# A token copy scaled by routing weights: four output pools become one output tile used in regions

## The chip, the cores and the metric

The kernel runs on one core of a Trainium2 chip. The metric is device time in microseconds (us) of one execution, as the median of several runs. One more execution of each kernel was recorded by the hardware profiler; all profile lines here come from such executions, and times in them are counted from the start of the span.

Three engines matter. VectorE (DVE) and ScalarE (ACT) compute. SyncE (SP) computes nothing here; it issues transfers. Transfers run on 16 DMA engines, fed by two queues in this kernel: ScalarE's queue (q10 in the profile) loads x, SyncE's queue (q1) loads the weights and stores the results.

## The reference

```python
def reference(x, expert_indices, expert_weights):
    batch, seq, hidden = x.shape              # 16, 1024, 512, float32
    k = expert_indices.shape[-1]              # 2
    x_expanded = x[:, :, np.newaxis, :].repeat(k, axis=2)
    weights = expert_weights[..., np.newaxis]
    return (x_expanded * weights).astype(np.float32)
```

Every token has a row of 512 numbers and two weights, and the result holds the row twice, once times each weight. The expert indices are used for their shape only. 33.6 MB of x and 0.1 MB of weights go in, and 67.1 MB come out.

## The kernel before

There are 16,384 tokens, which is 128 rows of tokens for each of the 128 partitions. The kernel works on five tiles of 25 token rows (`groups`) and a remainder of 3 (`LAST`). In a tile each partition holds 25 consecutive tokens, so a partition's part of a transfer is one contiguous run in memory: 2 KB per row of input and 4 KB per row of output.

*Loads.* `load` brings a tile of x into one of two buffers (`x_pool`). Tile 0 comes in five loads of 4, 4, 5, 8 and 4 rows; the others come in one load of 25 rows. The three loads of weights are issued on SyncE's queue beside the first three loads of x; the last three rows of x (`z_tile`) are loaded behind tile 0. Tiles 0 and 1 are loaded at the start, and tile i+2 after the products of tile i have been written into the program. As these loads stand on ScalarE's queue, they are issued in order with ScalarE's products, and they wait until both engines have read the old tile in that buffer.

*Products.* `product` has two forms. On VectorE one TENSOR_TENSOR instruction makes up to four rows (`CH`), with x and the weights both broadcast. On ScalarE one ACTIVATE makes half an output row: 512 numbers times one weight. For the first two pieces of tile 0 a third form splits single half-rows between ScalarE and VectorE (`nc.any`), two of three to VectorE as TENSOR_SCALAR.

*Stores.* Each tile is made in four pieces of 7, 6, 6 and 6 rows (`PIECES`). Piece h is written to a tile of its own pool, `o_pools[h]`, each with one buffer; VectorE makes the first four rows, ScalarE the others, and SyncE then stores the piece. So piece h of the next tile can be filled only when the store of piece h of this tile has landed. The remainder uses the buffer of piece 0 and is stored last, in a transfer of 3 rows. In all there are 21 stores, 10 loads of x and 3 of weights.

The framework places the waits: an instruction waits for the semaphores of what last wrote or read its bytes. Each engine runs its own instructions in program order.

Of the kernel before, what the change touches and what calls it, by code (L numbers as in the profile page):

```python
# [1 line left out]

# [4 lines left out]


@with_exitstack
def kernel(  # L10
    ctx: ExitStack,
    tc: tile.TileContext,
    x: bass.AP,
    expert_indices: bass.AP,
    expert_weights: bass.AP,
    out: bass.AP,
):
    nc = tc.nc

    batch, seq, hidden = x.shape  # L20
    k = expert_weights.shape[-1]
    P = nc.NUM_PARTITIONS
    ntok = batch * seq
    assert ntok % P == 0
    A_TOTAL = ntok // P

    f32 = mybir.dt.float32
    row = k * hidden
    CH = 4


    groups = [25, 25, 25, 25, 25]
    TX = max(groups)
    LAST = 3
    assert sum(groups) + LAST == A_TOTAL

    xf = x.rearrange("b s h -> (b s) h")
    of = out.rearrange("b s k h -> (b s) (k h)")
    wf = expert_weights.rearrange("b s k -> (b s) k")

    w_pool = ctx.enter_context(tc.tile_pool(name="w_pool", bufs=1))
    x_pool = ctx.enter_context(tc.tile_pool(name="x_pool", bufs=2))
    o_pools = [
        ctx.enter_context(tc.tile_pool(name=f"o_pool{h}", bufs=1)) for h in range(4)
    ]

    w_tile = w_pool.tile([P, A_TOTAL * k], f32)

    def rows(of_all, done, T):
        return of_all[done * P : (done + T) * P, :].rearrange(  # L50
            "(p a) n -> p (a n)", a=T
        )


    if LAST:
        z_pool = ctx.enter_context(tc.tile_pool(name="z_pool", bufs=1))
        z_tile = z_pool.tile([P, LAST * hidden], f32)

    tiles = []
    done = 0  # L60
    for n in groups:
        tiles.append((done, n))
        done += n

    loaded = []

    def load(i):
        if i >= len(tiles):
            return
        done, n = tiles[i]  # L70
        x_tile = x_pool.tile([P, TX * hidden], f32)
        src = rows(xf, done, n)
        steps = [4, 4, 5, 8, 4] if i == 0 else [n]
        for e, step in enumerate(steps):
            at = sum(steps[:e])
            nc.scalar.dma_start(
                out=x_tile[:, at * hidden : (at + step) * hidden],
                in_=src[:, at * hidden : (at + step) * hidden],
            )
            if i == 0 and e < 3:  # L80
                weights(e)
        if i == 0 and LAST:
            nc.scalar.dma_start(out=z_tile, in_=rows(xf, A_TOTAL - LAST, LAST))  # L83
        loaded.append(x_tile)


    T0 = groups[0]
    G = len([n for n in groups[1:] if n == T0])
    head = (1 + G) * T0

    def weights(e):
        if e == 0:
            nc.sync.dma_start(out=w_tile[:, : T0 * k], in_=rows(wf, 0, T0))
        elif e == 1:
            nc.sync.dma_start(
                out=w_tile[:, T0 * k : head * k].rearrange("p (g n) -> p g n", g=G),
                in_=wf[T0 * P : head * P, :].rearrange(
                    "(g p a) n -> p g (a n)", g=G, p=P
                ),
            )  # L100
        else:
            nc.sync.dma_start(
                out=w_tile[:, head * k :], in_=rows(wf, head, A_TOTAL - head)
            )

    def product(engine, o_tile, t, x_in, c, m):

        o = t * row
        if engine is not None:
            for e in range(m * k):  # L110
                out_e = o_tile[:, o + e * hidden : o + (e + 1) * hidden]
                in_e = x_in[:, e // k * hidden : (e // k + 1) * hidden]
                w_e = w_tile[:, c + e : c + e + 1]
                if engine is nc.scalar or engine is nc.any and (c + e) % 3 == 2:
                    nc.scalar.mul(out=out_e, in_=in_e, mul=w_e)  # L115
                else:
                    nc.vector.tensor_scalar(  # L117
                        out=out_e,
                        in0=in_e,
                        scalar1=w_e,  # L120
                        scalar2=None,
                        op0=mybir.AluOpType.mult,
                    )
            return
        nc.vector.tensor_tensor(  # L125
            out=o_tile[:, o : o + m * row].rearrange(
                "p (t k h) -> p t k h", t=m, k=k
            ),
            in0=x_in[:, : m * hidden]
            .rearrange("p (t h) -> p t h", t=m)  # L130
            .unsqueeze(2)
            .to_broadcast([P, m, k, hidden]),
            in1=w_tile[:, c : c + m * k]
            .rearrange("p (t k) -> p t k", t=m)
            .unsqueeze(3)
            .to_broadcast([P, m, k, hidden]),
            op=mybir.AluOpType.mult,
        )

    def make(i, e, o_tile, x_in, c, m):  # L140
        if i == 0 and e < 2:
            product(nc.any, o_tile, 0, x_in, c, m)
            return
        v = min(m, CH)
        product(None, o_tile, 0, x_in, c, v)
        if m > v:
            product(nc.scalar, o_tile, v, x_in[:, v * hidden :], c + v * k, m - v)

    PIECES = [7, 6, 6, 6]
    for i in range(2):  # L150
        load(i)
    for i, (done, n) in enumerate(tiles):
        x_tile = loaded[i]
        outr = rows(of, done, n)
        at = 0
        for h, m in enumerate(PIECES):
            o_tile = o_pools[h].tile([P, m * row], f32)
            make(
                i,
                h,  # L160
                o_tile,
                x_tile[:, at * hidden : (at + m) * hidden],
                (done + at) * k,
                m,
            )
            nc.sync.dma_start(out=outr[:, at * row : (at + m) * row], in_=o_tile)  # L166
            at += m
        load(i + 2)
    if LAST:
        o_tile = o_pools[0].tile([P, PIECES[0] * row], f32)  # L170
        product(None, o_tile, 0, z_tile, (A_TOTAL - LAST) * k, LAST)
        nc.sync.dma_start(
            out=rows(of, A_TOTAL - LAST, LAST), in_=o_tile[:, : LAST * row]
        )

# [1 line left out]
_INS = ['x', 'expert_indices', 'expert_weights']  # L177
_OUTS = [((16, 1024, 2, 512), 'float32')]


# [23 lines left out]
```

## Time and profile before

| what | us |
|---|---|
| median of 3 runs | 240.68 |
| the 3 runs | 240.57, 240.68, 242.03 |
| the profiled execution | 240.69 |
| its span in the profile | 238.9 |
| VectorE busy | 90.3 |
| ScalarE busy | 57.3 |

The span goes from the first to the last instruction that the profiler recorded; the 1.8 us between it and the execution's time lie outside. The page counts as busy only instructions that compute. The DMA rows give the mean share of the 16 DMA engines that had a packet under way, and the bytes moved. A packet is counted in the stretch in which it is seen, so a short stretch can show a share above 1.00 and a rate that jumps; long stretches are to be read.

The store queue of this kernel issues its first store at 16.28 us and the last one, of 3 rows, at 215.68 us.

### The profile page before, as it was taken

The numbers are of one execution on the slowest core, as the hardware profiler recorded it, in microseconds if no ns is written. First come the engines' busy times: TensorE is split into PE (matmuls) and PEld (weight loads), VectorE is DVE, ScalarE is ACT, GpSimd is POOL, SyncE is SP. The second block draws the span as 40 slices with busy tenths as digits, with TensorE's granted clock in tenths as the row PEclk, the third lists the DMA queues.
The fourth block names the chain that finished last, engine by engine and source line by source line (L and its number), as shares of the span: only waits on it lengthen the run. The fifth ranks groups of instructions, "written<-read, shape, count | busy, mean of one in ns | idle before, by whom it ended". The sixth has DMA issues, their size and how long they took to land.

```text
span 238.9 us, 260 instructions
## 1 busy us (share of the span) xinstructions
DVE 90.3 (38%) x37; ACT 57.3 (24%) x89; POOL 0.2 (0%) x4
## 2 busy tenths in 40 slices
DVE  0769300060074557000775260035575556741000
ACT  0747000060034226000444150042245423400000
POOL 0000000000000000000000000000000000000000
DMA  6999999899899999999999999999999999999995
GB/s 242 428 409 413 445 441 460 383 457 483 378 438 399 460 418 447 424 440 430 411 444 447 494 406 406 414 429 436 433 437 428 432 440 429 446 418 428 432 426 245
DMA packets 5281, 100.80 MB, mean 422 GB/s; under 512 B 1312, under 2 KB 1312, under 8 KB 1440
## 3 DMA queue, kind: packets, MB, share of 16 engines
q1 hardware_dynamic: 3840, 67.24, 65.5%
q10 hardware_dynamic: 1440, 33.56, 33.0%
q14 instruction: 1, 0.01, 0.0%
HBM read 33.69 MB, written 67.11 MB: 422 GB/s over the span
## 4 chain that ended last, share of the span: by engine, by line
DMA 81%; DVE 9%; issue 0%; ACTq 0%; DVEq 0%; SPq 0%
DMA out_dram<-o_tile 60%; DMA x_tile<-in_x_dram 20%; DVE o_tile L125 9%; ACTq L83 0%; DVEq L125 0%; SPq L166 0%
## 5 line engine op out<-in xcount | busy, mean ns | idle before, releaser
L125 DVE TENSOR_TENSOR o_tile<-x_tile,w_tile 128x4096 f32<-128x4096 f32 x18 | 79.6, 4425 | 113.6 <-DMA out_dram<-o_tile 87.7
L115 ACT ACTIVATE o_tile<-x_tile,w_tile 128x512 f32<-128x512 f32 x88 | 56.0, 709 | 142.2 <-DMA out_dram<-o_tile 110.9
L117 DVE TENSOR_SCALAR o_tile<-x_tile,w_tile 128x512 f32<-128x512 f32 x18 | 7.4, 481 | 7.7 <-DMA x_tile<-in_x_dram 7.7
L125 DVE TENSOR_TENSOR o_tile<-z_tile,w_tile 128x3072 f32<-128x3072 f32 x1 | 3.4, 3358 | 4.1 <-DMA out_dram<-o_tile 4.1
L115 ACT ACT_TABLE_LOAD x1 | 1.3, 1283 | 6.9 <-DMA x_tile<-in_x_dram 6.9
L188 POOL MEMSET const-bfloat16-1.0<- 128x1 bf16 x1 | 0.1, 102 | 0.0
L188 POOL MEMSET const-uint8-127<- 128x1 uint8 x1 | 0.1, 102 | 0.0
L188 POOL MEMSET const-float32-1.0<- 128x1 f32 x1 | 0.1, 99 | 0.0
L188 POOL MEMSET const-float32-0.0<- 128x1 f32 x1 | 0.1, 98 | 0.2 <-issue 0.2
## 6 DMA issues: line engine op xcount, KB each, us to landing
out_dram<-o_tile SPq DMA_DIRECT2D x15, 3072.0 KB, 40.8
x_tile<-in_x_dram ACTq DMA_DIRECT2D x4, 6400.0 KB, 35.2
out_dram<-o_tile SPq DMA_DIRECT2D x5, 3584.0 KB, 36.9
x_tile<-in_x_dram ACTq DMA_DIRECT2D x3, 1024.0 KB, 7.6
x_tile<-in_x_dram ACTq DMA_DIRECT2D x1, 2048.0 KB, 15.0
out_dram<-o_tile SPq DMA_DIRECT2D x1, 1536.0 KB, 21.9
x_tile<-in_x_dram ACTq DMA_DIRECT2D x1, 1280.0 KB, 10.5
z_tile<-in_x_dram ACTq DMA_DIRECT2D x1, 768.0 KB, 20.6
```

The lines of the kernel that those rows point to most:

```text
L115: nc.scalar.mul(out=out_e, in_=in_e, mul=w_e)
L117: nc.vector.tensor_scalar(out=out_e, in0=in_e, scalar1=w_e, scalar2=None, op0=mybir.AluOpType.mult,)
L125: nc.vector.tensor_tensor(out=o_tile[:, o : o + m * row].rearrange("p (t k h) -> p t k h", t=m, k=k), in0=x_in[:, : m * hidden] .rearrange ...
L188: nc = _bacc.Bacc("TRN2", target_bir_lowering=False, num_devices=1)
```

## The change

One tile `o_ring` of 25 output rows takes the place of the four pools, with the same bytes in all. Each tile of x writes its results at the same row numbers of `o_ring`, cut into pieces (`cuts`): rows 0 to 12 and 13 to 24 for the first two tiles, rows 0 to 8, 9 to 16 and 17 to 24 for the three others. The remainder is written to rows 0 to 2. That makes 14 stores in place of 21.

In each piece VectorE now makes about two thirds of the rows, in steps of up to four, and ScalarE the last third: 9 + 4 rows and 8 + 4 rows in the first two tiles; 6 + 3, 6 + 2 and 6 + 2 in the others; 2 + 1 in the remainder. The split by half-rows in tile 0 is gone.

Tile 0 is loaded in two transfers of 9 and 16 rows in place of five; the three loads of weights keep their order on SyncE's queue. There are 7 loads of x in place of 10, and 24 transfers in all in place of 34.

```diff
+    FIRST = [9, 16]
...
-    o_pools = [
-        ctx.enter_context(tc.tile_pool(name=f"o_pool{h}", bufs=1)) for h in range(4)
-    ]
+    o_pool = ctx.enter_context(tc.tile_pool(name="o_pool", bufs=1))
...
+    o_ring = o_pool.tile([P, TX * row], f32)
...
-        steps = [4, 4, 5, 8, 4] if i == 0 else [n]
+        steps = FIRST if i == 0 else [n]
...
-            if i == 0 and e < 3:
-                weights(e)
+            if i == 0 and e == 0:
+                for g in range(3):
+                    weights(g)
...
-    def make(i, e, o_tile, x_in, c, m):
-        if i == 0 and e < 2:
-            product(nc.any, o_tile, 0, x_in, c, m)
-            return
-        v = min(m, CH)
-        product(None, o_tile, 0, x_in, c, v)
-        if m > v:
-            product(nc.scalar, o_tile, v, x_in[:, v * hidden :], c + v * k, m - v)
+    def fill(o_tile, x_in, c, m):
+        v = m - m // 3
+        for t in range(0, v, CH):
+            u = min(t + CH, v)
+            product(None, o_tile, t, x_in[:, t * hidden : u * hidden], c + t * k, u - t)
+        product(nc.scalar, o_tile, v, x_in[:, v * hidden :], c + v * k, m - v)

-    PIECES = [7, 6, 6, 6]
+    def emit(src, dst, c, cuts):
+        for at, to in zip(cuts, cuts[1:]):
+            o_tile = o_ring[:, at * row : to * row]
+            fill(o_tile, src[:, at * hidden : to * hidden], c + at * k, to - at)
+            nc.sync.dma_start(out=dst[:, at * row : to * row], in_=o_tile)
+
     for i in range(2):
         load(i)
     for i, (done, n) in enumerate(tiles):
...
-        for h, m in enumerate(PIECES):
-            o_tile = o_pools[h].tile([P, m * row], f32)
-            make(
...
-            )
-            nc.sync.dma_start(out=outr[:, at * row : (at + m) * row], in_=o_tile)
-            at += m
+        cuts = [0, 13, n] if i < 2 else [0, 9, 17, n]
+        emit(loaded[i], rows(of, done, n), done * k, cuts)
         load(i + 2)
-    if LAST:
-        o_tile = o_pools[0].tile([P, PIECES[0] * row], f32)
-        product(None, o_tile, 0, z_tile, (A_TOTAL - LAST) * k, LAST)
-        nc.sync.dma_start(
-            out=rows(of, A_TOTAL - LAST, LAST), in_=o_tile[:, : LAST * row]
-        )
+    emit(
+        z_tile,
+        rows(of, A_TOTAL - LAST, LAST),
+        (A_TOTAL - LAST) * k,
+        [0, LAST],
+    )
```

More of the change, by code (lines that the diff above doesn't have):

```diff
@@ L152 @@
     for i, (done, n) in enumerate(tiles):
-        x_tile = loaded[i]
-        outr = rows(of, done, n)
-        at = 0
-        for h, m in enumerate(PIECES):
-            o_tile = o_pools[h].tile([P, m * row], f32)
-            make(
[L159 to L164, printed above, removed]
-            )
-            nc.sync.dma_start(out=outr[:, at * row : (at + m) * row], in_=o_tile)
-            at += m
-        load(i + 2)
-    if LAST:
-        o_tile = o_pools[0].tile([P, PIECES[0] * row], f32)
-        product(None, o_tile, 0, z_tile, (A_TOTAL - LAST) * k, LAST)
-        nc.sync.dma_start(
-            out=rows(of, A_TOTAL - LAST, LAST), in_=o_tile[:, : LAST * row]
-        )
+        cuts = [0, 13, n] if i < 2 else [0, 9, 17, n]
+        emit(loaded[i], rows(of, done, n), done * k, cuts)
+        load(i + 2)
+    emit(
[4 more added lines that the diff above has]
+    )
 _INS = ['x', 'expert_indices', 'expert_weights']
```

## The prediction

> **What bounds the kernel now.** I read the first page from the top: busy shares, the slices, the bytes, the chain of waits.
>
> ```profile
> span 238.9 us, 260 instructions
> DVE 90.3 (38%) x37; ACT 57.3 (24%) x89; POOL 0.2 (0%) x4
> DMA  6999999899899999999999999999999999999995
> ...
> q1 hardware_dynamic: 3840, 67.24, 65.5%
> q10 hardware_dynamic: 1440, 33.56, 33.0%
> ...
> HBM read 33.69 MB, written 67.11 MB: 422 GB/s over the span
> ...
> DMA 81%; DVE 9%; issue 0%; ACTq 0%; DVEq 0%; SPq 0%
> ```
>
> No compute engine is busy half the time. The DMA row holds nines and eights but for the two edges, and the queues' packets fill 65.5 + 33.0 = 98.5% of 16 engines' span. The waits say the same from the other side: VectorE and ScalarE wait for stores to leave, and the store queue waits for VectorE.
>
> ```profile
> ACT o_tile L115 <- DMA out_dram<-o_tile: 110.9, 15, 18.4
> DVE o_tile L125 <- DMA out_dram<-o_tile: 91.7, 16, 17.9
> ...
> SPq L166 <- DVE o_tile L125: 184.6, 18, 27.8
> ```
>
> That last row looks like compute holding stores back. It is not: while SP waits, earlier stores are still in flight. Windows decide it (columns: stretch, length, busy time of three engines, PE clock, DMA share, GB/s).
>
> ```profile
> 0.00:2.00 2.00, 0.00 (x0) 0.00 (x0) 0.20 (x4) 1.00 0.20 25
> 2.00:3.00 1.00, 0.00 (x0) 0.00 (x0) 0.00 (x0) 1.00 0.60 181
> 4.00:16.00 12.00, 7.39 (x18) 6.40 (x9) 0.00 (x0) 1.00 1.02 420
> 20.00:60.00 40.00, 10.37 (x3) 5.98 (x10) 0.00 (x0) 1.00 1.02 442
> 20.00:235.00 215.00, 80.11 (x19) 48.05 (x76) 0.00 (x0) 1.00 1.00 433
> 234.00:236.00 2.00, 0.00 (x0) 0.00 (x0) 0.00 (x0) 1.00 1.01 430
> 236.00:237.00 1.00, 0.00 (x0) 0.00 (x0) 0.00 (x0) 1.00 0.44 184
> ```
>
> From 20 to 235 us the share is 1.00 at 433 GB/s. So the span is the bytes at 433 GB/s (100.80 MB: 232.8 us) plus some 6.1 us of edges and of a slower start. The bytes are the same after the change. The time can move only if the DMA runs dry somewhere, if its rate changes, or if the edges do.
>
> **The change, part by part.** Units first: one token row of output for all partitions is 524,288 bytes, 1.21 us at 433 GB/s; one of input is half, 0.605 us.
>
> *Compute.* The rows that price it:
>
> ```profile
> L125 DVE TENSOR_TENSOR o_tile<-x_tile,w_tile 128x4096 f32<-128x4096 f32 x18 | 79.6, 4425 | 113.6 <-DMA out_dram<-o_tile 87.7 <-DMA x_tile<-in_x_dram 25.9
> ...
> L117 DVE TENSOR_SCALAR o_tile<-x_tile,w_tile 128x512 f32<-128x512 f32 x18 | 7.4, 481 | 7.7 <-DMA x_tile<-in_x_dram 7.7
> ...
> L115 ACT ACT_TABLE_LOAD x1 | 1.3, 1283 | 6.9 <-DMA x_tile<-in_x_dram 6.9
> ```
>
> ```profile
> 0.73 2.85 ACTq L76 DMA_DIRECT2D x_tile<-in_x_dram  x5
> 6.02 2.46 DVE L117 TENSOR_SCALAR o_tile<-x_tile,w_tile 128x512 f32<-128x512 f32 x6 [6.02 <-DMA x_tile<-in_x_dram]
> 16.28 192.34 SPq L166 DMA_DIRECT2D out_dram<-o_tile  x20
> 49.58 3.78 ACT L115 ACTIVATE o_tile<-x_tile,w_tile 128x512 f32<-128x512 f32 x6 [27.38 <-DMA x_tile<-in_x_dram]
> ```
>
> VectorE makes four rows in 4.43 us, 1.11 a row; ScalarE makes six half-rows in 3.78 us, 0.63 each, 1.26 a row. After the change VectorE makes 17 rows of each of the first two tiles, 18 of each later one and 2 of the last three: 90 rows, 100 us. ScalarE makes 38 rows, 48 us. Both stay far under the span, so only the places count where a store waits for them.
>
> *The start.* The first load grows from 4 rows to 9. Four rows landed at 6.02, so nine land at 6.0 + 5 x 0.605 = 9.1, and the other sixteen at 18.8. VectorE's nine rows run from 9.1 to 19.0. ScalarE's first rows need the second load: 18.8 + 1.28 (table) + 8 x 0.63 gives 25.1. So the first store leaves at about 25.2 where it left at 16.28: 9 us later. What hides this is the load queue: x tile 0, the last three rows and x tile 1 are 53 input rows, 32.1 us, issued on ScalarE's queue ahead of its products. From 2.6 us on they last until about 34.7, so there are 9.5 us to spare; with that cover gone, each us of a later store would cost one.
>
> *The start's rate.* 4 to 16 us ran at 420 rather than 433 GB/s, a loss of 12 x 13/433 = 0.36 us. The row allows two readings. If the small first loads cause it, two loads in place of five give up to 0.36 us back. If reading without stores causes it, reading alone lasts 9 us longer and costs 9 x 13/433 = 0.27 us. I take zero, between them. The Trainium skill ("DMA: Bandwidth & Descriptors", in its section on the iDMA fabric) measured a load stream alone at 408.7 GB/s; by that figure the longer reading would cost an estimated 0.5 us. The trace's 420 lies above it and decides.
>
> *Packets.* Loads are 10 transfers and q10 holds 10 x (128 + 16) = 1440 packets: one for each partition's whole run, and one per engine at the end. Ten transfers fewer are 1440 packets fewer, 90 on each engine.
>
> ```profile
> q1 hardware_dynamic: 787, 0.13, 4.4%
> ...
> q10 hardware_dynamic: 150, 6.81, 65.7%
> q1 hardware_dynamic: 148, 3.49, 33.7%
> ```
>
> The first row is from 0 to 17 us, where q1 carries the tiny weight packets: 0.044 x 17 x 16 / 787 = 15 ns each. So at most 90 x 15 ns = 1.35 us go. The other two rows, from 26 to 50 us, say that it is less: loads (51 KB a packet) make 6.81 MB in 0.657 of 24 us, 432 GB/s, stores (24 to 28 KB) 3.49 MB in 0.337, also 432. A price of 15 ns on each would part these rates by 0.7%. I take 0.2 us off, nearer to that row, and keep 0 and 1.35 for the range.
>
> *Shares and loads.* In that window 150 load packets alternate with 148 store packets, so each queue's share goes by packet size. Store packets grow to 53 and 49 KB beside loads of 51 KB: loads fall from two thirds of the rate to half. Working forward row by row at 433 GB/s, x tiles 1 to 4 land near 44, 74, 121 and 161 us. The regions that they fill come free at about 57, 101, 138 and 183, so every load stays at least 13 us early.
>
> *The regions.* Three in place of four (two at first) mean fewer stores queued while the next is made. A region's fill starts when the store that held it has landed, and must end before what is still queued runs out. From a load's issue to its landing goes 5.3 us (0.73 to 6.02), of which 4 rows' data take 2.4; so a hand-over costs 2.9 us at most beside the fill. The two tightest places are those without a load in flight:
> - Tile 1's second piece, about 81 us: one store of 13 rows is queued, 15.7 us, and the fill of 8 rows takes 8.9. That leaves 6.9, and after the 2.9, 4.0 us.
> - Tile 2's second piece, about 127 us. Its last rows overlap the old 12-row region, so they wait for that store. Nine rows are queued, 10.9 us; two rows on either engine take 2.6. That leaves 8.3, and 5.4.
>
> Elsewhere two stores or a load stand behind. So SP's longer waits at each store cost nothing, and nothing else is queued behind them on SP. ScalarE's queue also carries the x loads, each behind the products of the tile before: issued about 3 us later than now (near 90 and 136 us in place of 86.96 and 132.63), which the 13 us cover.
>
> ```profile
> 86.96 0.36 ACTq L76 DMA_DIRECT2D x_tile<-in_x_dram  x1
> ...
> 132.63 0.35 ACTq L76 DMA_DIRECT2D x_tile<-in_x_dram  x1
> ```
>
> *The end.* The last three rows wait for the first region of tile 4; then 16 rows, 19.4 us, are still queued, and two rows on VectorE take 2.2. The last store is of the same size, so the tail (data until 236.5, the end at 238.9) stays.
>
> *Sum.* The profiled execution took 240.69, 1.8 above its span and equal to the median of 240.68. 240.69 + 0 - 0.2 = 240.5.
>
> **The rivals.**
> 1. *The queue runs dry at the two tight hand-overs (slower).* It decides when a landing and re-issue take over 6.9 us in place of 2.9, which engines out of step would do, since a store lands with its slowest engine. At 10 us the places lose 3.1 + 1.7: 245.3. For it: only one store is in flight there. Against it: at the end all engines stop between 236 and 237 us, so they keep within 1 us.
> 2. *Long store packets move more slowly (slower).* No store above 28 KB a packet is in the trace. At 420 GB/s, the lowest rate above, 67.11 MB take 4.8 us longer: 245.3. Against it: loads of 51 KB run at the stores' rate.
> 3. *A gap at each transfer goes (faster).* The rate of 442 from 20 to 60 us, held for all 215, would save 4.4 us: 236.3. The Trainium skill ("DMA: Bandwidth & Descriptors", on the anatomy of one DMA) gives about 2.0 us fixed for a transfer on the GpSimd path; ten in series would be 20 us, 220.7. That sum the trace refutes here, because transfers overlap. In the last stage the fills, each begun by a landing, follow at 7.28 and 7.26 us, and 6 rows in 7.26 us are 433 GB/s with no room for a gap:
>
> ```profile
> 189.25 2.56 ACT L115 ACTIVATE o_tile<-x_tile,w_tile 128x512 f32<-128x512 f32 x4 [3.44 <-DMA out_dram<-o_tile]
> ...
> 196.53 2.56 ACT L115 ACTIVATE o_tile<-x_tile,w_tile 128x512 f32<-128x512 f32 x4 [4.72 <-DMA out_dram<-o_tile]
> ...
> 203.79 2.56 ACT L115 ACTIVATE o_tile<-x_tile,w_tile 128x512 f32<-128x512 f32 x4 [4.69 <-DMA out_dram<-o_tile]
> ```
>
> 4. *The tile is not tracked by regions.* Then each fill would wait for all stores, and the DMA would idle for it: nine pieces of tiles 2 to 4 at 6.6 us of fill and 2.9 us each are 86 us, of which two loads of 15.1 us cover 30: 296. The built program's waits speak against it: each fill waits for the store that held its own rows.
>
> **How the numbers follow.** Within 1% (238.3 to 243.1, about what a measurement of this kernel can tell from no change) is the forecast, 0.80. Rival 1 has 0.08, rival 2 0.05, rival 3 0.06, rival 4 0.01. So faster 0.06, same 0.80, slower 0.14. The forecast alone reaches from 240.7 - 1.35 - 0.36 = 239.0 to 240.7 + 0.27 = 241.0; the runs of before reached 242.0, so I end at 242.2. Outside lie the rivals, 0.20 at most.
>
> **What would show it.** The DMA row should stay at nines, with 1.00 of DMA share from 20 to 235 us; VectorE near 100 us busy, ScalarE near 48; the first store at 25 us; 3841 packets; x loads issued near 30, 90 and 136 us. A slice of 7 or less near 96 or 137 us would be rival 1. A rate other than 433 GB/s at a share of 1.00 would be rival 2 or 3.

## The result, and the profile after

The changed kernel takes 239.86 us (median of 13 runs, 239.59 to 240.33) where the kernel before takes 241.42 (13 runs, 240.41 to 242.53). The ratio is 0.9938, with a 95% interval of 0.9919 to 0.9956. Run again beside the experiments it took 239.89 against 240.73: 0.9959, interval 0.9940 to 0.9978. It is faster by about half a per cent, which the many runs tell from zero though it is under the 1% of the forecast. The fastest executions of the two differ by 0.82 us (240.41 and 239.59); the medians differ by 1.56, because the kernel before varies more, up to 242.53. What its longer executions lose is not shown: the one that was profiled took 240.69. Where a kernel below had executions more than 1.5% above its fastest, they are counted in its median but left out of its ratio.

The page of the changed kernel, with the rows that answer to those shown of before:

```profile
span 237.8 us, 214 instructions
DVE 99.1 (42%) x29; ACT 49.1 (21%) x77; POOL 0.2 (0%) x4
DMA  7999999999999999999999999999999999999996
...
q1 hardware_dynamic: 2832, 67.24, 65.7%
q10 hardware_dynamic: 1008, 33.55, 33.2%
...
DMA 68%; DVE 20%; issue 2%; ACT 1%; DVEq 0%; SPq 0%
```

Nines from edge to edge, 98.9% of the span in packets, VectorE at 99 and ScalarE at 49 us: the kernel is bound as before. The chain's share of VectorE rose from 9% to 20%, and yet the DMA share stays at 1.00: a chain through an engine is no loss while other transfers are queued. The windows (stretch, length, three engines' busy time, PE clock, DMA share, GB/s):

```profile
4.00:16.00 12.00, 7.11 (x2) 0.00 (x0) 0.00 (x0) 1.00 1.05 447
20.00:60.00 40.00, 7.50 (x2) 9.98 (x17) 0.00 (x0) 1.00 1.01 428
20.00:235.00 215.00, 88.00 (x26) 47.94 (x77) 0.00 (x0) 1.00 1.00 431
26.00:50.00 24.00, 1.50 (x1) 3.99 (x7) 0.00 (x0) 1.00 0.98 413
```

These rates need care. The view counts a packet whole where it is seen, and here the engines run in step: one load packet more or less on each of the 16 is 0.82 MB, or 34 GB/s over 24 us. With each packet shared out over its recorded time, 4 to 16 us have 430 GB/s (418 before) and 26 to 50 us 426 (433 before), so both differences are smaller than the rows make them. The stretch from 26 to 50 us shows something else that was not expected. First the queues from 26 to 50 us (packets, MB, share), then the weights' loads (KB, us from issue to landing):

```profile
q10 hardware_dynamic: 209, 9.88, 97.6%
q1 hardware_dynamic: 209, 0.02, 0.7%
```

```profile
w_tile<-in_expert_weights_dram SPq DMA_DIRECT2D x1, 100.0 KB, 36.8
w_tile<-in_expert_weights_dram SPq DMA_DIRECT2D x1, 25.0 KB, 5.3
w_tile<-in_expert_weights_dram SPq DMA_DIRECT2D x1, 3.0 KB, 50.4
```

The stores' queue moved 0.02 MB in 24 us, though its first store had been issued at 25.12. Equal packet counts say why: an engine takes one packet from each queue in turn. The records show it directly: every 1.90 us each engine starts one load packet and one tiny packet. (The Trainium skill, "DMA: Bandwidth & Descriptors", section on queues, rings and completion order, has engines go round their queues in this way, switching only after a whole packet; by that rule, the 209 beside 209 agrees.) The weights are 768 packets of 24 and 200 bytes, 48 on each engine, and stand ahead of the stores. Each waits for a load packet of up to 51 KB. Before, tile 0 came in many short packets, and the same three loads landed 3.9, 15.0 and 17.4 us after their issue. Now 3 KB take 50.4 us, and no store moves until then. The engines do not run dry meanwhile, because the load queue stays full that long: tile 2 of x was issued at 30 us.

Where the 1.1 us between the two profiled spans (of executions of 240.69 and 239.60) went follows from the records of single packets. The median durations are:

```
bytes in a packet    12288   24576   28672   32768   49152   51200   53248
ns                     460     912    1062    1213    1815    1891    1966
9 ns + bytes at 27.22 GB/s
                       460     912    1062    1213    1815    1890    1965
```

So each packet costs 9 ns beside its bytes, and without that the 16 engines would move 436 GB/s. (The Trainium skill gives 435 GB/s as the ceiling, in the specifications of "DMA: Bandwidth & Descriptors"; the records agree.) Summed over the 16 engines and divided by 16, in us:

```
                                            before   after
first packet starts                           1.74    1.72
packets' time, mean of the engines          235.50  235.09
gaps between packets                          0.05   -0.14
last packet ends                            237.29  236.67
last landing                                237.62  237.01
from it to the end of the span                1.29    0.81
```

(A gap below zero means that packets overlap a little.) The packets' time fell by 0.4: 80 data packets and 10 completions fewer at 9 ns are -0.8. The rest is packets that took longer than the rule. The load of the last three rows gives -0.4: before, its packets took 286 ns in the mean for 235 by the rule, mostly between 18 and 20 us, where the stores start. Load packets of 51 KB give +0.7: from 20 to 48 us, without stores, they took 1,899 ns for 1,890, which is 0.1 in all, but the last one on each engine, just ahead of the first store, took 2,420 ns (0.5 us), and some from 96 to 108 us the rest. Tiny packets give +0.1, tile 0's loads nothing. The gaps give another -0.2 and the end of the program -0.5. These parts are read from two executions; no run below takes out one alone and shows it in the time.

### The profile page after: what moved, and what is told of

The parts are those of the page before. It is cut to its first block, busy times and chain, and to the rows that moved or that the text cites. A ratio compares the mean times of both kernels' runs of the same rounds, so it can differ in the third digit from the quotient of the medians.

```text
span 237.8 us, 214 instructions
## 1 busy us (share of the span) xinstructions
DVE 99.1 (42%) x29; ACT 49.1 (21%) x77; POOL 0.2 (0%) x4
## 4 chain that ended last, share of the span: by engine, by line
DMA 68%; DVE 20%; issue 2%; ACT 1%; DVEq 0%; SPq 0%
DMA out_dram<-o_ring 65%; DVE o_ring L126 20%; DMA x_tile<-in_x_dram 3%; ACT o_ring L116 1%; DVEq L126 0%; SPq L152 0%
## 5 line engine op out<-in xcount | busy, mean ns | idle before, releaser
L126 DVE TENSOR_TENSOR o_ring<-x_tile,w_tile 128x4096 f32<-128x4096 f32 (+2 forms) x28 | 96.8, 3507 | 113.0 <-DMA out_dram<-o_ring 99.9
L116 ACT ACTIVATE o_ring<-x_tile,w_tile 128x512 f32<-128x512 f32 x74 | 46.5, 708 | 139.2 <-DMA out_dram<-o_ring 130.8
L116 ACT ACT_TABLE_LOAD x1 | 1.3, 1283 | 18.8 <-DMA x_tile<-in_x_dram 18.8
L126 DVE TENSOR_TENSOR o_ring<-z_tile,w_tile 128x2048 f32<-128x2048 f32 x1 | 2.3, 2292 | 4.3 <-DMA out_dram<-o_ring 4.3
L116 ACT ACTIVATE o_ring<-z_tile,w_tile 128x512 f32<-128x512 f32 x2 | 1.3, 713 | 8.3 <-DMA out_dram<-o_ring 8.3
```

Of the source, the lines that this page charges most:

```text
L126: nc.vector.tensor_tensor(out=o_tile[:, o : o + m * row].rearrange("p (t k h) -> p t k h", t=m, k=k), in0=x_in[:, : m * hidden] .rearrange ...
```

## The experiments

Times in this section are medians; each ratio is against executions of the kernel before that were taken beside it, so ratios are to be compared rather than times of different groups of runs.

**Tile 0 in two loads, alone** (in the kernel before)

```diff
-        steps = [4, 4, 5, 8, 4] if i == 0 else [n]
+        steps = [9, 16] if i == 0 else [n]
...
-            if i == 0 and e < 3:
-                weights(e)
+            if i == 0 and e == 0:
+                for g in range(3):
+                    weights(g)
```

> The kernel before with tile 0 in two loads (9 and 16 rows) and the weights' loads issued behind the first of them; pools, pieces and the 21 stores stay. The start (larger first packets): the 4 to 16 us stretch rises from 420 to about 447 GB/s and nearly the whole gain appears, about 0.9 to 1.5 us less than before. The number of stores: at most 0.3 us of gain. The order of reading and writing (in the changed kernel the weights' tiny packets alternate with large load packets, so stores begin only at 50 us and reads and writes hardly overlap until then): the same gain as by the start, since stores are held back here too; the inline run parts the two.

Measured: 240.75 us against 240.70, ratio 0.9988 (0.9968 to 1.0007). No gain that can be told. Yet the row from 4 to 16 us did rise to 446 GB/s (430 shared out, as in the changed kernel), and the stores were held back too (the first landed at 60.36 us):

```profile
4.00:16.00 12.00, 4.84 (x12) 5.07 (x7) 0.00 (x0) 1.00 1.04 446
...
26.00:50.00 24.00, 4.05 (x1) 0.00 (x0) 0.00 (x0) 1.00 0.98 413
```

The 413 is 426 when shared out, again as in the changed kernel. By the records the load of the last three rows is 0.4 us shorter here than in the kernel before, and the last load packet of each engine ahead of the first store takes 2,391 ns, which costs 0.5. So the start and the order of reading and writing, taken together, are not the gain; the run does not part them. The engines stay in step: the first store's landings are 0.84 us apart, the last one's 0.64.

**Five loads in the changed kernel**

```diff
-    FIRST = [9, 16]
+    FIRST = [4, 4, 5, 8, 4]
...
-            if i == 0 and e == 0:
-                for g in range(3):
-                    weights(g)
+            if i == 0 and e < 3:
+                weights(e)
```

> The changed kernel with tile 0 in the five loads of before (4, 4, 5, 8, 4 rows, weights beside the first three). The start: the gain is lost, about 1 us slower than the changed kernel (some 240.9 to 241.4), first stretch back at 420 GB/s. The number of stores: gain kept, about 239.9. The order of reading and writing: lost too, as stores begin near 25 us.

Measured: 252.35 us, ratio 1.0463 (1.0416 to 1.0511). No theory had foreseen a loss of 12 us. Its page and windows:

```profile
span 249.7 us, 216 instructions
```

```profile
26.00:50.00 24.00, 0.00 (x0) 0.00 (x0) 0.00 (x0) 1.00 0.99 383
96.00:102.00 6.00, 5.37 (x2) 1.54 (x3) 0.00 (x0) 1.00 0.80 346
20.00:235.00 215.00, 86.17 (x26) 42.39 (x68) 0.00 (x0) 1.00 0.99 415
```

Two things are to be seen. From 26 us on the share is full and the rate is 383 (384 shared out): packets take longer. Near 100 us the share itself falls to 0.80: some engines have nothing to do. Two rows from 40 to 50 us show the first: 36 load packets in 0.478 of 16 x 10 us are 2.12 us each, where 1.89 is the rule.

```profile
q10 hardware_dynamic: 36, 1.84, 47.8%
q1 hardware_dynamic: 34, 1.81, 45.1%
```

The completion records show the second. Each transfer completes once per engine; this is when the first and the last of the 16 engines completed it, in us:

```
                     first store     second store    third store     last store
changed kernel       66.79 - 67.60   81.28 - 82.11   98.97 -101.58  236.31 -237.01
five loads           50.68 - 57.62   80.82 - 92.51   98.41 -113.39  243.65 -248.73
kernel before        35.57 - 43.13   57.92 - 65.45   74.41 - 75.08  236.70 -237.62
```

With five loads the engines are 7 to 15 us out of step on these stores, and 5 us at the end. A store lands with its slowest engine, so the next fill starts late, and the engines that are ahead run dry. In the sums, packets take 241.8 us of each engine (8.0 above the rule, 1.5 in the changed kernel) and 4.9 us are gaps. Of these some 3.0 lie at the end, where engines are done before the slowest (0.3 in the changed kernel). The kernel before is out of step by 7.5 us at first, is back within 0.7 us at its third store, and shows no such loss.

**Four pieces in the changed kernel**

```diff
-        cuts = [0, 13, n] if i < 2 else [0, 9, 17, n]
+        cuts = [0, 7, 13, 19, n]
```

> The changed kernel with the four pieces of before (7, 6, 6, 6 rows) for every tile: 21 stores in place of 14. The start and the order: gain kept, within 0.2 us of the changed kernel, about 239.9. The number of stores: seven more, each 0.1 to 0.2 us, so about 1 us slower, near 240.9.

Measured: 243.09 us, ratio 1.0076 (1.0048 to 1.0104). The number of stores explains at most 0.6 us of the 3.2 above the changed kernel (56 packets and 7 completions at 9 ns). The rest again is out of step: the weights' last 3 KB landed at 36.27 us on the first engine and at 52.57 on the last, and the last store's landings are 3.8 us apart. At the end the engines are done 2.9 us before the slowest in the mean, for 0.3 in the changed kernel, which is most of the loss. But the sizes alone do not do it: the run with two loads alone has the same loads, 21 stores of the same sizes and the same weights ahead of them. There the weights' last 3 KB landed at 51.23 us on the first engine and at 51.97 on the last, and the time was 240.75. Its four pools, its split of the work and the first store's issue (13.19 us there, 14.53 here) differ; which of them decides was not tested.

**Weights off the stores' queue, in the changed kernel** (`queue` is the engine that `weights` now issues from)

```diff
-            if i == 0 and e == 0:
-                for g in range(3):
-                    weights(g)
+            if i == 0 and e == 0:
+                weights(0, nc.sync)
+            if i == 0 and e == 1:
+                weights(1, nc.scalar)
+                weights(2, nc.scalar)
```

> The changed kernel with the second and third loads of weights issued on ScalarE's queue behind tile 0's second load, so that no tiny packets stand ahead of the stores. The first store then moves data from about 25 us on, not from 50, and lands near 57 in place of 67.6. The start: time unchanged, about 239.9. The order of reading and writing: the gain shrinks, about 0.5 to 1.5 us slower than the changed kernel.

Measured: 240.49 us, ratio 0.9980 (0.9959 to 1.0001). The first store landed at 60.14, so it did move early. Whether the time rose against the changed kernel is not clear: this interval lies just above the first one of the changed kernel (0.9919 to 0.9956) and overlaps the second (0.9940 to 0.9978). Long loads and long stores alternate here from 25 us on, with all engines within 0.9 us until 82 us, and the rate is 423 GB/s from 26 to 50 us, shared out. So early long stores alone are not what cost 12 us.

**The changed kernel again**

> The changed kernel itself, as the mark for the others of this call: about 0.8 to 1.5 us under the kernel before.

Measured: 239.89 us, ratio 0.9959 (0.9940 to 0.9978), as expected.

**Without the third form of products** (in the kernel before)

```diff
-        if i == 0 and e < 2:
-            product(nc.any, o_tile, 0, x_in, c, m)
-            return
```

> The kernel before without the third form of products: all pieces of tile 0 are made as in the other tiles, so VectorE has 21 instructions of products in place of 37; all transfers stay. In the traces so far the time from the last landing to the span's end is 1.28 and 1.23 us where the third form is used and 0.77 to 0.98 us where it is not; VectorE's last instruction comes late. The end of the program: about 0.4 us less than before, near 240.3, with that stretch at 0.8 us. If it is the number of transfers or the ring that shortens the end, the time stays at 240.7 and the stretch at 1.25 us.

Measured: 240.46 us, ratio 0.9990 (0.9966 to 1.0013), and 0.9 us from the last landing to the end. This fits the theory, but a later run (each store in two) breaks it: that kernel keeps the third form and also ends 0.9 us after its last landing. In the kernel before and in the run with two loads alone, VectorE's very last instruction is late by some 0.35 us; why only there stays open.

**Five loads, weights off the stores' queue** (the five loads of above, and the second and third loads of weights on ScalarE's queue behind the third of them)

```diff
-    FIRST = [9, 16]
+    FIRST = [4, 4, 5, 8, 4]
...
+            if i == 0 and e == 2:
+                weights(1, nc.scalar)
+                weights(2, nc.scalar)
```

> The changed kernel with tile 0 in five loads (252.35 us so far), and with the second and third loads of weights on ScalarE's queue behind tile 0's third load, so that no tiny packets stand on the stores' queue. Engines out of step (the tiny packets leave the 16 engines at different places when the first store comes, and long load and store packets then hold each other up): the loss of 12 us goes, time 239.9 to 240.8, and all engines land a transfer within about 1 us. Early long stores beside loads, whatever the engines' order: still about 250 us.

Measured: 241.56 us, ratio 1.0020 (0.9997 to 1.0042), with ten executions from 240.27 to 242.36 and two at 252.99 and 253.83. Most of the loss went, so the tiny packets are a part of its cause, but not the whole: the engines still get out of step as soon as the first store comes (its landings are 5.3 us apart in an execution of 241.03), and two executions of twelve lost as much as before. The profiled one ran at 431 GB/s from 26 to 50 us, shared out, so long packets out of step are not slow as such. Why two executions lost is not shown, since neither was profiled.

**Each store of the kernel before in two**

```diff
-            nc.sync.dma_start(out=outr[:, at * row : (at + m) * row], in_=o_tile)
+            half = (m + 1) // 2
+            nc.sync.dma_start(
+                out=outr[:, at * row : (at + half) * row], in_=o_tile[:, : half * row]
+            )
+            nc.sync.dma_start(
+                out=outr[:, (at + half) * row : (at + m) * row],
+                in_=o_tile[:, half * row :],
+            )
```

> The kernel before with each of the 20 stores of pieces issued as two transfers: 41 stores in place of 21, so 160 more packets on each engine. Packet records of the traces fit 9 ns plus bytes at 27.2 GB/s for each packet. The price of a packet: 160 x 9 ns = 1.4 us slower than before, near 242.1. No price (packets overlap): no change, 240.7. A price for each transfer of 0.1 us or more: 2 us slower or more.

Measured: 243.12 us, ratio 1.0084 (1.0056 to 1.0112), so 2.0 us by the ratio. The packets' time rose from 235.5 to 238.8: 160 packets and 20 completions at 9 ns are 1.6, and load packets above the rule 1.55 more; smaller gaps and a shorter end gave 1.1 back. The price is there, and each packet's duration is the rule's; the sum of 1.4 was too small, since it left out the load packets, which took longer here. Why they did was not tested.

**Five loads, first store late**

```diff
-    FIRST = [9, 16]
+    FIRST = [4, 4, 5, 8, 4]
...
-    def emit(src, dst, c, cuts):
-        for at, to in zip(cuts, cuts[1:]):
-            o_tile = o_ring[:, at * row : to * row]
+    def emit(src, dst, c, cuts, up=0):
+        for at, to in reversed(list(zip(cuts, cuts[1:]))):
+            o_tile = o_ring[:, (at + up) * row : (to + up) * row]
...
+        up=TX - LAST,
```

> The changed kernel with tile 0 in the five loads of before, and with the pieces of every tile stored in reversed order (rows 13 to 24 first, and the last three rows made in ring rows 22 to 24). So the loads are those of the run at 252.35 us, but the first store waits for the last of them and starts near 26 us, when the queue of loads moves the long packets of tile 1. The first store meeting short load packets is the cause: 239.8 to 240.8 us, engines land the first stores within 1 us of each other. The five loads as such are the cause: near 252, or some executions there.

Measured: 240.69 us, ratio 0.9974 (0.9950 to 0.9998). Ten executions lie between 239.79 and 241.57, two at 244.39 and 244.81; none is near 252. One of the two was profiled, and even there the first store, issued at 25.89, landed on all engines within 0.33 us and the second within 0.47. Its loss came after 90 us. So the five loads as such do not make the loss; it takes an early first store as well. What this store meets is not parted here: at 25.89 us the short load packets are past, and so are the tiny packets, whose last landed at 18.45. The run with five loads and the weights off the stores' queue gives the tiny packets the larger part. An early store beside short loads may add that a small difference between engines is one packet or two, and so a whole store of 53 KB more or less; that was argued, not measured.

**Four pieces, weights off the stores' queue**

```diff
-        cuts = [0, 13, n] if i < 2 else [0, 9, 17, n]
+        cuts = [0, 7, 13, 19, n]
...
+            if i == 0 and e == 1:
+                weights(1, nc.scalar)
+                weights(2, nc.scalar)
```

> The changed kernel with the four pieces of before (243.09 us so far), and with the second and third loads of weights on ScalarE's queue, so that the first store, made at about 15 us, is not held back behind tiny packets. Tiny packets holding stores back at different lengths on different engines cost the 3 us: near 240.6, which is the changed kernel plus 56 packets of 9 ns and 7 completions. Smaller stores with two loads cost them in another way: it stays near 243.

Measured: 241.10 us, ratio 1.0006 (0.9987 to 1.0025): 2.0 us less than with the weights on the stores' queue (1.7 by the ratios), 0.5 above the expectation. Holding stores back behind tiny packets, unequally on different engines, was most of those 3 us. Here two of the early stores land 10.3 us apart, and that costs little, since the engines come back: from 81 us on no transfer's landings are more than 3.5 us apart, and the last store's are 1.6.

**Two pieces for all tiles**

```diff
-        cuts = [0, 13, n] if i < 2 else [0, 9, 17, n]
+        cuts = [0, 13, n]
```

> The changed kernel with two pieces (13 and 12 rows) for all five tiles: 11 stores in place of 14. The price of a packet: 24 data packets and 3 completions fewer on each engine, 0.25 us less, about 239.6. A hand-over that runs dry: the reserve by the prediction's rows is 14.5 us queued less 10.0 us of fill less 2.9 us, 1.6 us, at each of six hand-overs of tiles 2 to 4; if it is overrun the time rises by the overrun at each, 1 us or more in all.

Measured: 240.13 us, ratio 0.9961 (0.9940 to 0.9982), the same as the changed kernel. The packets' time is 234.80, 0.2 to 0.3 less, as expected, but gaps (0.3 us in place of about none) and a longer end of the program (1.0 us in place of 0.8) take it back. No hand-over ran dry:

```profile
20.00:235.00 215.00, 84.34 (x23) 51.30 (x82) 0.00 (x0) 1.00 1.00 430
```

**The regions alone** (five loads and four pieces in the changed kernel)

```diff
-    FIRST = [9, 16]
+    FIRST = [4, 4, 5, 8, 4]
...
-        cuts = [0, 13, n] if i < 2 else [0, 9, 17, n]
+        cuts = [0, 7, 13, 19, n]
```

> The changed kernel with tile 0 in five loads and with the four pieces of before, so that of the change only the one tile used in regions and the split of a piece between the engines are left. It completes a square: two loads with large pieces 239.9, two loads with four pieces 243.1, five loads with large pieces 252.4. The size of the stores makes the run at 252 (load packets of 51 KB alternating with store packets of 49 and 53 KB, out of step): here, with store packets of 24 and 28 KB, 240.3 to 241.0, as before. The regions or the split make it: 245 or more.

Measured: 240.73 us, ratio 0.9987 (0.9959 to 1.0015). With five loads and four pieces, regions and split cost nothing. The square, in us:

```
                  4 pieces (24 and 28 KB)   2 and 3 pieces (32 to 53 KB)
five loads               240.73                     252.35
two loads                243.09                 239.86, 239.89
```

In the kernel with regions neither half of the change gains by itself: against the upper left one loses 2.4 and the other 11.6 (2.1 and 11.5 by the ratios). Together they gain. The square does not hold for the four pools, where two loads with four pieces took 240.75: the sizes alone do not decide whether the engines get out of step.

## Why the prediction was right

It said 240.5, 239.0 to 242.2, and no change beyond 1%; it was 239.86, a change of 0.6% by the ratio. The mechanism was right: the same bytes through DMA engines that stay full. Of what it left out, 0.6 us are in its term for packets and 0.5 at the end of the program. Step by step:

- *The bound.* Right. The share is 1.00 from 20 to 235 us before and after, so compute, waits and the number of regions do not show in the time.
- *Compute and the start.* Right to 0.3 us: the first nine rows landed at 8.89 (9.1), the other sixteen at 18.7 (18.8), the first store left at 25.12 (25.2), and the loads of tiles 2 to 4 at 30.02, 91.04 and 136.53 (30, 90, 136).

```profile
8.89 18.61 DVE L126 TENSOR_TENSOR o_ring<-x_tile,w_tile 128x4096 f32<-128x4096 f32 x5 [8.89 <-DMA x_tile<-in_x_dram]
...
25.12 191.68 SPq L152 DMA_DIRECT2D out_dram<-o_ring  x14
30.02 0.37 ACTq L76 DMA_DIRECT2D x_tile<-in_x_dram  x1
...
91.04 0.36 ACTq L76 DMA_DIRECT2D x_tile<-in_x_dram  x1
...
136.53 0.35 ACTq L76 DMA_DIRECT2D x_tile<-in_x_dram  x1
```

- *The cover of the late store.* The conclusion held, its working did not. It counted 9.5 us to spare between the first store at 25.2 and the end of the loads at 34.7. In fact stores moved nothing before 50 us, and what covered them was tile 2's load, issued at 30.02, before tile 1's landed at 36.05. The step had priced the weights' loads by their own time and not by their place ahead of the stores. The cover had to last 25 us longer than worked out, and that it did was luck.
- *The start's rate.* Zero was close, but neither reading of the 420 GB/s holds. The loads of tile 0 took 0.49 us more than the packet rule before and 0.46 after. Loads of 51 KB without stores beside them took 1,899 ns for 1,890, 0.1 us in all. The 420 is mostly the price of packets: by the rule, packets of 8 to 16 KB run at 423 to 429 GB/s, and 665 packets under 512 bytes took 0.6 us of each engine in that stretch. What moved was at the point where the stores start: 0.4 us gone in the load of the last three rows, 0.5 us new in the last load packet ahead of the first store.
- *Packets.* Mis-sized. It took 0.2 us off; 80 data packets and 10 completions at 9 ns are 0.8. The two window rates of 432 GB/s, worked out from figures of three digits and from packets counted whole at the edges, could not part 431 from 433, which is what 912 ns for 24,576 bytes and 1,891 ns for 51,200 make. The range had kept 1.35 as its end.
- *Shares and loads.* Wrong in the times, right in the result. Tiles 1 to 4 landed at 36.1, 51.9, 125.7 and 165.6 us (forecast 44, 74, 121, 161), and their regions came free at 67.6, 101.6, 138.4 and 183.8 (57, 101, 138, 183). Each load was at least 12.7 us early.
- *The hand-overs.* Right: no stretch near 96 or 137 us fell. The run with two pieces for all tiles, whose reserve is 1.6 us by the same rows, kept its share of 1.00 too.
- *The end.* It was to stay; it fell by 0.5 us, for a reason that is open.
- *The rivals.* The first, engines out of step, did not happen in the changed kernel, where landings stayed within 2.6 us of each other from the first store on. But its mechanism is real: with five loads DMA engines did run dry (share 0.80 near 100 us), as a part of 12 us. That the engines stop within 1 us in the trace of before, the argument against it, says nothing of another start. The second, long store packets, is refuted as such: 53,248 bytes take 1,966 ns, on the line of the others. The third needed a gap at each transfer; the records show 9 ns at each packet, and twenty more transfers cost 2.0 us in all, where the Trainium skill's 2.0 us for each ("DMA: Bandwidth & Descriptors", anatomy of one DMA, for another path) would make an estimated 40. The fourth is refuted by the fills, which started as their own rows' store landed: 67.72 us after 67.60, 82.20 after 82.11, with later stores still under way.

## What to carry to other kernels

Where the DMA engines are full, count packets before transfers: each costs 9 ns here, whatever its length, so longer runs gain a little. What is worth far more is that all engines stay in step. Try changes of load sizes and of store sizes together, since in this kernel one of them lost 12 us without the other, and look at when the first and the last engine complete a transfer; also look what tiny transfers stand ahead of large ones on their queue.

## What the runs showed of the hardware that was not expected

- A queue of tiny packets beside a queue of long ones advances by one tiny packet per long one. 3 KB of weights took 50.4 us to land, and the stores behind them waited as long.
- The 16 engines of one core can get out of step by 5 to 15 us, and with five loads they were still 5 us apart at the end. A transfer lands with its slowest engine, and at the end the others wait: 2.9 us in the mean with two loads and four pieces, some 3.0 with five loads and large pieces.
- Long loads (51 KB) and long stores (49 and 53 KB) out of step can slow down to 384 GB/s at a full share (five loads, 26 to 50 us, each packet shared out over its time). That is not the rule: without the tiny packets ahead of the stores, five loads ran at 431 over the same stretch, their landings 5.3 us apart. In step it was 423, and out of step with stores of 24 and 28 KB 433 (the kernel before). Why the packets then take longer is not known from these runs.
- The last load packet of 51 KB on each engine ahead of the first store packet took 2.2 to 2.5 us in the mean, for 1.89: in the changed kernel and its second profile, in the runs with two loads alone and with two pieces for all tiles, and, 20 us earlier, in the changed kernel with the weights off the stores' queue. Why is not known.
